# Bias rows, block sums, score rows and value banks moved in a hybrid attention and HGRN2 layer

## The chip, the cores and the metric

One core of a Trainium2 chip runs the whole layer. The metric is the device time of one execution in microseconds; before and after are compared by the median of several runs. TensorE (PE) does the products and transposes, VectorE (DVE) and ScalarE (ACT) the elementwise work, GpSimd (POOL) a few powers and the issue of some DMAs, and SyncE (SP) issues most DMAs.

## The reference

One decoder layer for x of shape (1, 1024, 1024) in float32. Cut to its core:

```python
mod = silu(c) @ w_ada + b_ada
shift, scale, gate = split(mod, 3)
h = rmsnorm(x, norm_g) * (1 + scale) + shift
q_a, k_a, v_a, z_a, q_b, f_b, i_b, z_b, g_a, g_b = split(h @ w_in)
o_a = dilated_attention(q_a, k_a, v_a, rel_bias) * silu(z_a)      # 8 heads of 64
o_b = rmsnorm(hgrn2(silu(q_b), f_b, i_b, lb), onorm_g) * silu(z_b)  # 8 heads of 128
y = sigmoid(g_a) * (o_a @ w_branch_a) + sigmoid(g_b) * (o_b @ w_branch_b)
out = rmsnorm(x + gate * (y @ w_out), final_g)
```

The attention is causal softmax attention over three dilated windows, whose outputs are merged by the weights of their softmax denominators. The kernel does this as one softmax over all earlier keys, with a bias (a bucketed `rel_bias` plus the logarithm of how many windows hold the key) that depends on the distance alone.

## The kernel before, in words

Every fp32 product is done as three fp32r products of high and low parts (`mm3`: hi x hi, lo x hi, hi x lo). h, transposed, stands in four blocks: `b11`, `b12` (upper half of the rows, first and second half of the tokens), `b21`, `b22` (lower half). Most projections go in pairs of column blocks by a Strassen-like scheme (`add_pair`: seven steps of four products of three matmuls each instead of eight), for which four sums of blocks, `t1` to `t4`, are made beforehand.

**The order of work.** PE runs in the order of the program throughout. ACT, DVE and POOL are ordered by a planner with its own costs, which may put a later instruction ahead of an earlier one when the earlier waits; the exception is a `region` at the start, in which these engines also keep the order of the program. The planner may put instructions from outside the region between those inside.

**The start (L629 to L719).** x is loaded in eight tiles. `norm_x(t)` (ACT square sum, DVE, POOL power) and `scale_x(t)` (DVE) prepare a tile; `turn_x(j, th)` transposes (PE) and copies (ACT and DVE in turn). `bias_row(b)` makes a third of the bias table by a product, `bias_add(b)` adds the logarithm on DVE, and after the third the table is stored by a DMA that ACT issues (L624). `modulate(c)` makes scale and shift of two row blocks j (PE, ACT, DVE); `make_h(j, th)` writes h's high part (ACT) and low part (DVE). `first_products(j)` adds row block j to the first three projections (q, k and v of heads 0 and 1), in six banks; `split_first(n)` makes the high and low parts of their weights in one of four buffers. `sum_1(k)` makes a slice of `t1`; `sums(k)` makes slices of `t2`, `t3` and `t4` in place and destroys what `sum_1(k)` reads. At the end `FIRST[u][1]` (`ev_q`, `ev_k`, `ev_v`) copies the banks out and stores q and k; the region closes ahead of that.

**The stream.** All other projections are `stream` steps. A step is 12 matmuls in four quarters; `stream.ahead` splits the weights of the next two steps. `fill(n)` runs as many quarters as n times `fill.rate`, up to step `fill.limit`; what the limit holds back is owed. The first two steps (`first`) are another pair of v columns, and the transposes of v come between them.

**Attention (L753 to L876).** The 32 items are (head h, row pair j), j = 0 to 3. `load_head(h)` loads q, k, v and the bias of a head. `begin(n)` is a generator that does `score(h, i)` for the two rows of item n, one for each `next`: per chunk of up to 512 keys two products into one of two banks `pss`, a DVE operation that adds the bias and finds the maximum, and then exp (ACT), reciprocal and scaling (DVE). Meanwhile the item before is worked off: for m = 0 to j `turn(h, j, m)` transposes probabilities into `pt` and splits them to `pth` and `ptl`, and one turn later `value(h, j, m)` multiplies them with v into `po`; after the last m ACT and DVE copy `po` out. Filler is placed between, weighted by `ATT_W[j]`:

```python
if j < 3 or m > 1:
    fill(0.15 * w); next(nxt, None); fill(0.3 * w)
    if j in (0, 3):
        next(nxt, None)
    fill(0.25 * w)
```

So with j = 0 and 3 both rows of the next item are begun at one m, with j = 1 and 2 at m = 0 and m = 1. Row 7 of a head also calls `load_head(h + 1)`.

**After it.** Eight loads of the attention output are gated by `z` and split into `oah` and `oal`, with `fill(6)` after each, up to step `in_gating` (14 steps past `in_attention`, which is step 85). Then comes the branch product `m<-oah`, and the recurrence with more of the stream.

Of the kernel before, what the change touches and what calls it, by code (L numbers as in the profile page):

```python
# [10 lines left out]
F32 = mybir.dt.float32  # L11
# [8 lines left out]
P = 128  # L20
# [43 lines left out]
RAW = 6  # L64
CT = 7
AHEAD = 2
ATT_W = (2.4, 1.3, 0.9, 0.7)


class Stream:  # L70
# [104 lines left out]
def hybrid_layer(ctx: ExitStack, tc: tile.TileContext, x, w_ada, b_ada, w_in, w_branch_a, w_branch_b, w_out,  # L175
# [45 lines left out]
    fill = Filler(stream)  # L221
# [262 lines left out]
    with ExitStack() as st:  # L484
# [16 lines left out]
        region = ExitStack()  # L501
# [59 lines left out]
        def split_first(n):  # L561
            hi, lo = (wpool.tile([P, 4, P], F32R, name=name) for name in ("w_hi", "w_lo"))
            nc.scalar.copy(hi, stream.tiles[ids[n]])
            sub(lo, stream.tiles[ids[n]], hi)
            stream.done(ids[n])
            firsts[n] = hi, lo
# [49 lines left out]
        def bias_row(b):  # L616
            pb = pbs[b] = pm.tile([NH, 384], F32, name=f"pm{b}_0")
            nc.tensor.matmul(pb, rb, oh[:, 384 * b:384 * b + 384], start=True, stop=True)

        def bias_add(b):  # L620
            sl = slice(384 * b, 384 * b + 384)
            nc.vector.tensor_tensor(lc[:, sl], pbs[b], lc[:, sl], ALU.add)
            if b == 2:
                nc.scalar.dma_start(toep_d, lc)  # L624
# [16 lines left out]
        junk = lp.tile([P, D], BF16, name="junk")  # L641
        rows = [lp.tile([P, 256], F32, name=f"row{a}") for a in range(2)]

        for b in range(3):
            bias_row(b)
        norm_x(0)
        norm_x(1)
        scale_x(0)
# [1 line left out]
        scale_x(1)  # L650
        norm_x(3)
        scale_x(2)
        for b in range(3):
            bias_add(b)
        norm_x(4)
        scale_x(3)
        for j in range(4):
# [10 lines left out]
        for j in range(KT):  # L668
            turn_x(j, 1)
        split_first(0)  # L670
        modulate(0)
        load_wa(2)
        main = {(u, th): pm.tile([P, 512], F32, name=f"pm{u}_{th}") for th in range(2) for u in range(3)}
        make_h(0, 0)
        split_first(1)
        make_h(0, 1)
# [4 lines left out]
            first_products(0, us=(u,))  # L681
        modulate(1)
        load_wa(3)
        first_products(1)
        for j in (2, 3):
            for th in range(2):
                make_h(j, th)
        split_first(3)
        sum_1(0)
        sum_1(1)  # L690
        first_products(2)
        modulate(2)
        modulate(3)
        lx.close()
        add_blocks(hctx.enter_context(tc.tile_pool(name="hpool2", bufs=1, reuse_waits="tile")),
                   "b21", "b22", "t2", "t3", "t4")
        first_products(3)
        for th in range(2):
            make_h(4, th)
        split_first(4)  # L700
        split_first(5)
        for u in range(3):
            first_products(4, us=(u,))
        for j in (5, 6, 7):
            for th in range(2):
                make_h(j, th)
            if j < 7:
                sum_1(j - 3)
        first_products(5)
        stream.issue()  # L710
        first_products(6)
        region.close()
        stream.ahead(0)
        for u in range(3):
            first_products(KT - 1, us=(u,))
            for th in range(2):
                FIRST[u][1](main[u, th], th, True)
        for k in range(4):
            sums(k)  # L719
    again = dict(space=PSUM, reuse_waits="tile")  # L720
# [32 lines left out]
    with ExitStack() as at:  # L753
        ap1 = at.enter_context(tc.tile_pool(name="att1", bufs=1, **right))
        ap2 = at.enter_context(tc.tile_pool(name="att2", bufs=2, **right))
        psS = at.enter_context(tc.tile_pool(name="ps_s", bufs=2, **again))
        psO = at.enter_context(tc.tile_pool(name="ps_o", bufs=1, **again))
        heads = {}

        def load_head(h):  # L760
# [50 lines left out]
            sub(ptl[:, :w], pt[:, :w], pth[:, :w])  # L811
            return pth, ptl

        pos = {}

        def value(h, j, m, parts):
            vq, hh = heads[h][4], h % 2
            if m == 0:
                pos[h, j] = psO.tile([P, 256], F32, name="po")
            po = pos[h, j]  # L820
            for kk in range(2):
                kt = 2 * m + kk
                c0, n = kk * 256, (256 if kt <= 2 * j else P)
                for a, src in enumerate(parts):
                    nc.tensor.matmul(po[:, 256 - n:256], vq[:, kt], src[:, c0:c0 + n],  # L825
                                     start=kt == 0 and a == 0, stop=kt == 2 * j + 1 and a == 1)
            if m == j:
                t1 = ap1.tile([E, 256], F32, name="t1")
                oa = ap2.tile([E, 256], F32, name="oa")
                nc.scalar.copy(t1, po[E:2 * E])  # L830
                nc.vector.tensor_tensor(oa, po[0:E], t1, ALU.add)
                nc.sync.dma_start(oa_d[h // 2][E * hh:E * hh + E, 256 * j:256 * j + 256], oa)
# [19 lines left out]
                value(*late.pop(0))  # L852

        load_head(0)
        fill.limit = in_attention
        fill.rate = in_attention * 4 / NH / sum((j + 1) * w for j, w in enumerate(ATT_W))
        for _ in begin(0):
            fill(1.0)
        for n, (h, j) in enumerate(items):
            nxt = begin(n + 1)  # L860
            for m in range(j + 1):
                late.append((h, j, m, turn(h, j, m, rows[n])))
                w = ATT_W[j]
                if j < 3 or m > 1:
                    fill(0.15 * w)
                    next(nxt, None)
                    fill(0.3 * w)
                    if j in (0, 3):
                        next(nxt, None)
                    fill(0.25 * w)  # L870
                else:
                    fill(0.7 * w)
                run_late(1)
                fill(0.3 * w)
            rows.pop(n)
# [462 lines left out]
```

## Time and profile before

| | before |
|---|---|
| median of 3 runs | 1184.62 us (1182.9 to 1187.39) |
| profiled execution | 1183.43 us, span 1181.7 us |
| PE busy | 1118.6 us, 95% of the span |
| DVE busy | 820.2 us, 69% |
| ACT busy | 561.0 us, 47% |
| DMA | 189.53 MB, mean 160 GB/s |

PE does nearly all that lies on the way to the end. Rows of the profile name an engine, a line of the kernel, and the tiles as out<-in; what stands in brackets is how long the engine had been idle and what ended that. The tile names that matter here: `pm` the six banks of the first products, `pss` scores, `pt` transposed probabilities, `po` value products, `s` a row of probabilities, `m` a product of the stream. In rows of busy time by stretch the columns are the stretch, its length, the busy time of PE, its weight loads, DVE, ACT and POOL (with their instructions), the granted PE clock, and the share and rate of the DMA engines. The execution has four places that the change touches: the start (0 to 91 us), the begin of attention (to 118 us), attention (to 476 us) and the gating behind it (to 517 us).

### The profile page before, as it was taken

What the parts mean: (1) busy time and instruction counts of PE and PEld (TensorE: products, weight loads), DVE (VectorE), ACT (ScalarE), POOL (GpSimd) and SP (SyncE); (2) the same over time, 40 slices, a digit from 0 to 9 for tenths busy, and PEclk for the clock granted to TensorE, in tenths of its full rate; (3) what the DMA queues carried; (4) which work ended last, traced back from release to release, by engine and by line L of the source; (5) the groups of instructions that cost most, each with busy time, mean ns of one, the idle gap of its engine ahead of it and who ended that gap; (6) DMA issues with size and microseconds to landing.
All of it is one profiled execution on the core that took longest, in us unless ns stands there. A gap on an engine that the chain in (4) does not pass through costs nothing.

```text
span 1181.7 us, 21561 instructions
## 1 busy us (share of the span) xinstructions
PE 1118.6 (95%) x8250; PEld 913.3 (77%) x8250; DVE 820.2 (69%) x1636; ACT 561.0 (47%) x1092; POOL 69.8 (6%) x114
## 2 busy tenths in 40 slices
PE   4998999999999998999999999999999999999997
PEld 2766878877887787878877878788787877888886
DVE  4586878877777777654778797878878673668052
ACT  4454655578898886431343434344443433223021
POOL 2001101001011010000000000000000012000000
PEclk9798999999999999999999999999999999999998
DMA  9618567465365462766726254453525369874052
GB/s 315 206 50 227 150 180 168 145 170 147 97 147 149 115 148 72 243 192 216 224 66 197 82 178 135 126 171 90 188 82 171 111 218 307 287 226 153 19 178 72
DMA packets 157751, 189.53 MB, mean 160 GB/s; under 512 B 10656, under 2 KB 107040, under 8 KB 157648
## 3 DMA queue, kind: packets, MB, share of 16 engines
q1 hardware_dynamic: 149936, 162.34, 44.4%
q0 software_dynamic: 7296, 25.17, 8.6%
q8 instruction: 65, 1.06, 0.4%
q10 hardware_dynamic: 416, 0.65, 0.2%
q14 instruction: 38, 0.31, 0.1%
HBM read 129.36 MB, written 58.76 MB: 159 GB/s over the span
## 4 chain that ended last, share of the span: by engine, by line
PE 69%; issue 8%; DMA 8%; DVE 7%; ACT 6%; POOL 1%; SPq 0%; POOLq 0%; DVEq 0%; ACTq 0%
PE m L233 14%; PE m L235 13%; PE m L234 13%; PE pq L233 5%; PE pq L234 5%; PE pq L235 5%; DMA w_raw<-in_w_in_dram 4%; DMA k<-qk_d 2%; PE pp L978 2%; PE po L825 1%; PE pt L806 1%; ACT s L794 1%; DVE w_lo L218 1%; DMA x<-in_x_dram 1%; PE pou L1042 1%
## 5 line engine op out<-in xcount | busy, mean ns | idle before, releaser
L218 DVE TENSOR_TENSOR w_lo<-w_raw,w_hi 128x512 fp32r<-128x512 f32 x156 | 106.8, 687 | 41.9 <-ACT w_hi L240 40.3
L240 ACT CAST w_hi<-w_raw 128x512 fp32r<-128x512 f32 x146 | 90.2, 621 | 91.7 <-PE m L235 54.1
L316 ACT COPY ct<-m 128x512 f32<-128x512 f32 x90 | 52.6, 584 | 90.8 <-PE m L235 87.8
L240 ACT CAST w_hi<-w_s 128x512 fp32r<-128x512 f32 x90 | 56.0, 622 | 83.0 <-PE m L235 58.3
L263 DVE TENSOR_TENSOR ct<-m,ct 128x512 f32<-128x512 f32 x90 | 61.8, 686 | 20.0 <-PE m L235 19.5
L218 DVE TENSOR_TENSOR w_lo<-w_s,w_hi 128x512 fp32r<-128x512 f32 x90 | 61.8, 686 | 8.8 <-ACT w_hi L240 8.2
L794 ACT ACTIVATE s<-s,st 128x128 f32<-128x128 f32 (+3 forms) x64 | 49.7, 776 | 27.7 <-DVE st L791 27.4
L218 DVE TENSOR_TENSOR ptl<-pt,pth 128x512 fp32r<-128x512 f32 (+1 forms) x80 | 50.5, 632 | 16.8 <-ACT pth L810 16.4
L806 PE MATMUL pt<-kc,s 128*128 128x128 f32 x288 | 47.3, 277 | 11.0 <-DVE s L796 8.5
L810 ACT CAST pth<-pt 128x512 fp32r<-128x512 f32 (+1 forms) x80 | 43.1, 540 | 23.1 <-PE pt L806 20.7
L806 PEld LDWEIGHTS pt<-kc,s 128*128 128x128 f32 x288 | 35.8, 141 | 23.5 <-DVE s L796 12.3
L233 PE MATMUL m<-b21h,w_hi 128*128 128x512 f32 x124 | 52.3, 422 | 0.0
L233 PE MATMUL m<-b11h,w_hi 128*128 128x512 f32 x124 | 52.2, 421 | 0.0
L233 PE MATMUL m<-t4h,w_hi 128*128 128x512 f32 x120 | 50.4, 420 | 0.4 <-DVE ct L263 0.4
L233 PE MATMUL m<-b22h,w_hi 128*128 128x512 f32 x124 | 50.8, 410 | 0.0
L233 PE MATMUL m<-t1h,w_hi 128*128 128x512 f32 x120 | 50.1, 418 | 0.0
L233 PE MATMUL m<-t3h,w_hi 128*128 128x512 f32 x120 | 50.1, 418 | 0.0
L233 PE MATMUL m<-t2h,w_hi 128*128 128x512 f32 x120 | 49.6, 413 | 0.0
L235 PE MATMUL m<-b11l,w_hi 128*128 128x512 f32 x124 | 49.5, 399 | 0.0
L234 PE MATMUL m<-b11h,w_lo 128*128 128x512 f32 x124 | 49.2, 397 | 0.0
L235 PE MATMUL m<-b21l,w_hi 128*128 128x512 f32 x124 | 48.8, 394 | 0.0
L235 PE MATMUL m<-b22l,w_hi 128*128 128x512 f32 x124 | 48.7, 393 | 0.0
(333 smaller groups left out, 3186.2 us busy)
## 6 DMA issues: line engine op xcount, KB each, us to landing
w_raw<-in_w_in_dram SPq DMA_DIRECT2D x128, 256.0 KB, 3.2
wa<-in_w_ada_dram SPq DMA_DIRECT2D x16, 512.0 KB, 7.7
qk_d<-ct SPq DMA_DIRECT2D x32, 256.0 KB, 3.3
k<-qk_d POOLq DMA_DIRECT2D x32, 256.0 KB, 7.5
x<-in_x_dram SPq DMA_DIRECT2D x8, 512.0 KB, 9.3
toep<-toep_d SPq DMA_DIRECT2D x8, 512.0 KB, 9.4
qp<-qk_d POOLq DMA_DIRECT2D x16, 256.0 KB, 6.1
vq_d<-ct SPq DMA_DIRECT2D x32, 128.0 KB, 4.5
```

What stands on the lines that cost most here:

```text
L218: nc.vector.tensor_tensor(out_, a, hi.bitcast(F32), ALU.subtract)
L233: nc.tensor.matmul(ps, ah, bh, start=start, stop=False, skip_group_check=more)
L234: nc.tensor.matmul(ps, al, bh, start=False, stop=False, skip_group_check=more)
L235: nc.tensor.matmul(ps, ah, bl, start=False, stop=stop, skip_group_check=more)
L240: nc.scalar.copy(hi, src)
L263: nc.vector.tensor_tensor(out_, a, b_, op)
L316: nc.scalar.copy(c[name], b[which])
L794: nc.scalar.activation(s[:, :kw], s[:, :kw], AF.Exp, bias=prev, scale=-1.0, accum_out=st2[:, 2:3])
L806: nc.tensor.transpose(pt[:, c0:c0 + P], pn[b][:, kt * P:(kt + 1) * P], ident)
L810: nc.scalar.copy(pth[:, :w], pt[:, :w])
L825: nc.tensor.matmul(po[:, 256 - n:256], vq[:, kt], src[:, c0:c0 + n], start=kt == 0 and a == 0, stop=kt == 2 * j + 1 and a == 1)
L978: nc.tensor.matmul(pl[32 * b:32 * b + 32, c], kk[:, o:o + 32], qb[:, 2 - n:2, o:o + 32], start=True, stop=True)
```

## The change

1. The three `bias_row` go from ahead of `norm_x(0)` to behind the transposes of x and the first weight split, ahead of `modulate(0)`. The three `bias_add`, with the store of the table, go behind `modulate(0)`, ahead of the first `make_h`.
2. `sum_1(0)` goes behind `modulate(3)`; `sum_1(1)` to `sum_1(3)` go behind `first_products(6)` and `stream.ahead(0)`. `make_h` of each row block stands one product earlier, and the region closes only after the first products and their copies.
3. Both score rows of the next item are begun at one m (m = 0, or m = 2 for j = 3), with `fill(0.5)` between them. `ATT_W` grows for j = 0 and 1. The limit of the filler in attention is `in_gating`, and a `fill(1.0)` stands ahead of the first scores, with 0.5 instead of 1.0 after each of the two rows.
4. `po` is one tile of one bank for all items; item (h, j) takes the half j % 2.

```diff
-ATT_W = (2.4, 1.3, 0.9, 0.7)
+ATT_W = (2.6, 1.4, 0.9, 0.7)
...
-        for b in range(3):
-            bias_row(b)
         norm_x(0)
...
-        for b in range(3):
-            bias_add(b)
...
         split_first(0)
+        for b in range(3):
+            bias_row(b)
         modulate(0)
         load_wa(2)
+        for b in range(3):
+            bias_add(b)
...
         load_wa(3)
+        for th in range(2):
+            make_h(2, th)
         first_products(1)
-        for j in (2, 3):
-            for th in range(2):
-                make_h(j, th)
+        for th in range(2):
+            make_h(3, th)
         split_first(3)
-        sum_1(0)
-        sum_1(1)
         first_products(2)
...
-        first_products(3)
+        sum_1(0)
         for th in range(2):
             make_h(4, th)
+        first_products(3)
         split_first(4)
         split_first(5)
+        for th in range(2):
+            make_h(5, th)
         for u in range(3):
             first_products(4, us=(u,))
-        for j in (5, 6, 7):
-            for th in range(2):
-                make_h(j, th)
-            if j < 7:
-                sum_1(j - 3)
+        for th in range(2):
+            make_h(6, th)
         first_products(5)
+        for th in range(2):
+            make_h(7, th)
+        first_products(6)
         stream.issue()
-        first_products(6)
-        region.close()
         stream.ahead(0)
+        for k in (1, 2, 3):
+            sum_1(k)
         for u in range(3):
             first_products(KT - 1, us=(u,))
             for th in range(2):
                 FIRST[u][1](main[u, th], th, True)
+        region.close()
...
+        po2 = psO.tile([P, 2, 256], F32, name="po2")
...
-            if m == 0:
-                pos[h, j] = psO.tile([P, 256], F32, name="po")
-            po = pos[h, j]
+            po = po2[:, j % 2]
...
-        fill.limit = in_attention
+        fill.limit = in_gating
         fill.rate = in_attention * 4 / NH / sum((j + 1) * w for j, w in enumerate(ATT_W))
+        fill(1.0)
         for _ in begin(0):
-            fill(1.0)
+            fill(0.5)
...
-                if j < 3 or m > 1:
-                    fill(0.15 * w)
+                if m == (0 if j < 3 else 2):
                     next(nxt, None)
-                    fill(0.3 * w)
-                    if j in (0, 3):
-                        next(nxt, None)
-                    fill(0.25 * w)
+                    fill(0.5)
+                    next(nxt, None)
+                    fill(0.7 * w - 0.5)
```

More of the change, by code (lines that the diff above doesn't have):

```diff
@@ L670, in hybrid_layer @@
         split_first(0)
+        for b in range(3):
+            bias_row(b)
         modulate(0)
         load_wa(2)
-        main = {(u, th): pm.tile([P, 512], F32, name=f"pm{u}_{th}") for th in range(2) for u in range(3)}
+        for b in range(3):
+            bias_add(b)
+        main = {(u, th): pm.tile([P, 512], F32, name=f"pm{u}_{th}") for th in range(2) for u in (0, 1, 2)}
         make_h(0, 0)
@@ L812, in turn @@
             return pth, ptl
-        pos = {}
         def value(h, j, m, parts):
             vq, hh = heads[h][4], h % 2
-            if m == 0:
-                pos[h, j] = psO.tile([P, 256], F32, name="po")
-            po = pos[h, j]
+            po = po2[:, j % 2]
             for kk in range(2):
```

## The prediction

> **What bounds the kernel now.** I read the page first, then the busy time by stage, then who TensorE (PE) waits for in the two stages that the change touches most. All sums are against the profiled execution: 1183.43 us with a span of 1181.7 us, 1.2 us under the median of the three runs, 1184.62 us.
>
> ```profile
> span 1181.7 us, 21561 instructions
> PE 1118.6 (95%) x8250; PEld 913.3 (77%) x8250; DVE 820.2 (69%) x1636; ACT 561.0 (47%) x1092; POOL 69.8 (6%) x114
> ...
> 75.00:118.00 43.00, 35.11 (x144) 27.56 (x144) 32.72 (x64) 21.16 (x42) 4.34 (x8) 0.88 0.64 171
> 118.00:460.00 342.00, 327.11 (x1730) 272.74 (x1729) 259.95 (x605) 251.88 (x440) 25.72 (x48) 1.00 0.55 143
> 460.00:476.00 16.00, 12.53 (x70) 10.67 (x69) 10.10 (x20) 8.06 (x14) 0.00 (x0) 0.89 0.19 58
> 476.00:517.00 41.00, 40.56 (x186) 33.45 (x185) 28.74 (x46) 20.82 (x37) 0.00 (x0) 1.00 0.75 237
> ```
>
> PE is the bound, and the change removes no product, so only idle PE (63 us of the span) and time at the half clock can be won. Idle and in reach: 7.9 us before attention (first row of stages), 14.9 us in it, 3.5 us at its end. The waits of PE in the second of these stretches, and the main one of the third:
>
> ```profile
> PE pt L806 <- DVE s L796: 8.5, 9, 1.7
> PE po L825 <- DVE oa L831: 5.3, 2, 2.9
> PE pss L789 <- DMA k<-qk_d: 0.9, 2, 0.6
> ...
> PE pt L806 <- ACT ct L460: 2.5, 1, 2.5
> ```
>
> The reader sees two different illnesses: transposes of an item that come before its softmax is done (8.5 us), and, in the last line, attention running out of interleaved projection work.
>
> **1. Bias rows behind the transposes.** The start, in order of time:
>
> ```profile
> 11.83 3.99 PE L618 MATMUL pm<-oh,rb 32*8 32x384 f32 x6 [11.83 <-DMA oh<-in_onehot_dram]
> 15.86 0.55 DVE L622 TENSOR_TENSOR lc<-pm,lc 8x384 f32<-8x384 f32 x1 [0.73 <-PE pm L618]
> 16.82 1.06 ACT L554 ACTIVATE junk<-x 128x1024 bf16<-128x1024 f32 x1 [3.72 <-DVE lc L622]
> 18.89 0.47 PE L574 MATMUL pxt<-kc,x 128*128 128x128 f32 x1 [2.24 <-DVE x L559]
> 35.49 1.07 PE L532 MATMUL pmod<-wa,scz 128*32 128x256 f32 x16
> 38.76 0.81 ACT L580 ACTIVATE b11h<-xt,mods 128x512 fp32r<-128x512 f32 x1 [0.89 <-DVE mods L545]
> ...
> L517 SPq DMA_DIRECT2D x<-in_x_dram x1: 328/328/328, 3.4 to 3.4; - x1
> DMA to landing us min/median/max: 9.7/9.7/9.7
> ...
> 1061.22 1.72 PE pq L1221 x4
> ```
>
> The norm of the fifth x tile (16.82) stands on ScalarE (ACT) behind the store of the bias table, which waits for the last bias addition on VectorE (DVE). The tile itself, issued at 3.4, landed 9.7 us later, at 13.1. Freed, the chain norm, scale, transposes moves 3.7 us forward, to the end of the transposes. But the six products then stand between the transposes and `modulate(0)`: 3.99 us as in their row, or, at full clock, 6 x 0.32 = 1.9 us by the f32 product of the last line (four records of 512 columns in 1.72 us, 0.43 each). The clock rose here just as the transposes ended, so I take 2.4. The additions now stand on DVE behind `modulate(0)` (3 x 0.55 = 1.65 us), and the store's issue, 0.28 us, stands on ACT ahead of the first `make_h`, which PE's first product waits for. Sum: -3.7 + 2.4 + 1.65 + 0.28 = +0.6 us; ends -1.6 (additions hidden) and +2.2 (products at half clock).
>
> **2. `sum_1` behind the products, the region longer, filler ahead of the first scores.**
>
> ```profile
> 85.17 0.50 PE L593 MATMUL pm<-b21l,w_hi 128*128 128x512 f32 x1 [1.36 <-DVE b21l L218]
> 92.10 1.09 ACT L380 COPY ct<-pm 128x512 f32<-128x512 f32 x2
> 96.79 1.03 PE L439 MATMUL pt<-kc,ct 128*128 128x128 f32 x8
> 108.11 0.44 PE L788 MATMUL pss<-k,qp 128*128 128x128 f32 x1 [4.83 <-DMA k<-qk_d]
> ...
> 82.80:86.20 3.40, 1.70 (x5) 0.78 (x5) 3.40 (x8) 2.54 (x5) 0.00 (x0) 1.00 0.00 0
> 86.20:89.60 3.40, 2.77 (x7) 2.19 (x8) 3.06 (x6) 1.22 (x3) 0.00 (x0) 0.51 0.41 154
> 103.30:106.70 3.40, 0.00 (x0) 0.00 (x0) 2.37 (x4) 1.45 (x3) 0.00 (x0) 1.00 1.31 229
> 106.70:110.10 3.40, 1.36 (x4) 1.14 (x5) 0.30 (x2) 0.04 (x1) 0.00 (x0) 0.51 1.12 295
> ...
> 170.68 0.39 PE L234 MATMUL m<-t1h,w_lo 128*128 128x512 f32 x1
> 170.91 0.40 PE L235 MATMUL m<-t1l,w_hi 128*128 128x512 f32 x1
> ```
>
> With `sum_1` out of the way, `make_h(7)` comes before PE needs it: the waits around 85 (1.70 us idle in their 3.4 us stretch) and the half clock that follows them (0.51, so 1.7 us) go, and with the delay in resuming PE ends the first products about 4.5 us earlier. What is late next is the copy-out of q, k and v. It is now inside the hand-ordered region, behind `stream.ahead(0)`, whose second weight split needs a buffer that the last products' first third still reads, and behind three `sum_1` of some 2 us each (DVE, ACT, DVE in series; two 128x512 copies took 1.09 us above, so 0.6 to 0.7 us a step is an estimate). So the v copy (92.10 before) falls to about 96, the k stores likewise 2 us later, and PE, 4.5 us early at the v transposes (96.79), waits there. k lands about when it did, near 108. What remains is that `fill(1.0)` puts four quarter steps into the 4.83 us wait: 4 x 0.69 = 2.8 us won (a quarter is three 128x512 products, which start 0.23 us apart by the last two rows). The clock was 0.51 after this wait; 3.4 us of products at half clock lose 1.7 us, and I count 1.0 of them as won, since PE may still be idle enough for the clock to fall. Against it, only half as much filler stands behind the second row: 1.0 us of waiting. With 0.7 us for a slightly earlier k: -2.8 - 1.0 + 1.0 - 0.7 = -3.5 us. Ends: -7 (copies not late) and +5 (DVE does its sums first, k and weights late).
>
> On the clock the rows above show PE idle for 3.40 us, then 0.51 granted; but also 1.70 us idle of 3.40, then 0.51. The Trainium skill, "TensorE: Matmul & The Clock Gate", section "What's actually happening", puts the half clock after at least one idle window of about 3.4 us. By that rule the shortened wait would keep the full clock and win the other 0.7 us; the first pair of rows disagrees with it.
>
> **3. Both score rows at the first step.** For a third or fourth item this moves the second row from the next m to the same m.
>
> ```profile
> 172.28 0.39 PE L788 MATMUL pss<-k,qp 128*128 128x512 f32 x1
> 174.27 0.35 DVE L791 CUSTOM_DVE_ANT_0 s<-pss,toep,st 128x128 f32<-128x128 f32 x1
> 177.24 0.39 PE L788 MATMUL pss<-k,qp 128*128 128x512 f32 x1
> 181.96 0.55 PE L806 MATMUL pt<-kc,s 128*128 128x128 f32 x3 [0.50 <-DVE s L796]
> ...
> 217.46 0.39 PE L788 MATMUL pss<-k,qp 128*128 128x512 f32 x1
> 220.85 0.34 DVE L791 CUSTOM_DVE_ANT_0 s<-pss,toep,st 128x128 f32<-128x128 f32 x1
> ```
>
> Here the second row started 5.0 us after the first, and its softmax came 0.50 us late. Moved to 2.1 us after it (0.75 us of products, two quarters of 0.69), it is ready nearly 3 us sooner, more than the longest such wait, 1.7. Eight of the nine waits go: 7.5 us by their mean, and 1.0 us of resuming; one, at a head's first item, stays and grows, since 0.9 instead of 1.085 units of filler follow the second row there: +1.5. The next head's loads start earlier, too: -0.9 for the k waits.
>
> The price: a row of two chunks takes both score banks. The first row's second reduction ends 2.3 us after the row's start in the first case above, 3.7 in the other. The second row needs that bank at 2.1 + 0.5 = 2.6 us. So it waits 0 to 1.2 us, sixteen times (two items in eight heads): 0 to 19 us. Most rows lie near the first case; I take 0.3 each, +5. Sum: -8.5 + 1.5 - 0.9 + 5 = -2.9 us.
>
> **4. Two half banks for the value products.** Nothing, -1 at best, no loss that I see. The halves lie in one bank, and readers of a bank wait for all its writers:
>
> ```profile
> 670.77 0.39 PE L1059 MATMUL pou<-st,qb 128*128 128x128 f32 x2
> 672.11 0.39 PE L1059 MATMUL pou<-st,qb 128*128 128x128 f32 x2
> 672.60 0.28 ACT L1062 ACTIVATE jk<-pou 128x128 f32<-128x128 f32 x1 [2.37 <-PE pou L1059]
> ```
>
> ACT, idle for 2.37 us, wanted the first quarter of that bank, done at 671.2, and started only when the fourth was written. The 5.3 us of `po` waits (two) would stay. Even apart, `ptl` stood on the same blocked DVE queue in both. The Trainium skill, "PSUM — Partial Sum Buffer", section "PSUM bank collisions raise a hardware error", asks that engines be kept apart by bank and quadrant, not by address; this trace agrees by that 2.37 us. By addresses alone the halves would win up to 5.3 us.
>
> **5. More filler at the end, less after it.** The limit was 85 steps; attention's fill calls asked for (2 + 84) x 4.05 = 348 quarters where 83 x 4 = 332 were left. Now 89.2 x 3.90 = 348, and the limit is 14 steps on. So 16 quarters, 11 us, come into attention's tail. Its 3.5 us of idle and the clock of 0.89 over 16 us (1.8 us) are covered, with resuming some 6 us: -6 (ends -6.5 and -3).
>
> Those 11 us are then missing in the next stage:
>
> ```profile
> L218 DVE TENSOR_TENSOR oal<-oar,oah x8: 683/684/693, 481.9 to 508.5; 128x512 fp32r<-128x512 f32 x8
> ...
> L233 PE MATMUL m<-oah,w_hi x64: 392/397/477, 516.8 to 561.2; 128*128 128x512 f32 x64
> ```
>
> The gated attention output is whole at 509.2; PE asks for it at 516.8, 7.6 us of slack. Minus 11 that is -3.4 us of waiting; less crowded engines may finish the loads sooner: I take +2.5 (0 to +6).
>
> **Sum.** 0.6 - 3.5 - 2.9 + 0 - 6 + 2.5 = -9.3 us: 1183.4 - 9.3 = 1174.1, 1174 us. The weight `ATT_W` moves filler between items, not its total; its cost is inside term 3.
>
> **The rivals.**
> *Everything carries through.* Copies not late (-7 instead of -3.5), score banks free in time (0 instead of +5), `oal` keeps pace (0 instead of +2.5): 1174 - 11 = 1163 us. For it: DVE is busy only 260 of 342 us in attention. Against: its queue is in order, and one reduction took 3.7 us. Chance 0.20.
> *The gain before attention isn't one.* The longer region holds q, k and v; DVE, which has 32.7 us of work in 43, does it in a worse order and attention begins later: +5 instead of -3.5, so 1182 us. For it: the split that waits for the last products stands ahead of the copies on both engines. Against: PE arrives 4.5 us early, so that much of a delay costs nothing. Chance 0.24.
> *Slower: the second rows wait for the score banks.* Place: the first m of second and third items. With a mean wait of w the time is 1174 - 5 + 16 w, which passes 0.5% above today's at w = 1.34 us; at 1.4 us it is 1191 us. For it: the 3.7 us case, and two rows at once crowd DVE's queue further. Against: that case makes 1.1 to 1.2 us, and most rows end sooner. Chance 0.13.
> My forecast has 0.43.
>
> **How the numbers follow.** A difference under 0.5%, 5.9 us, can't be told from none: faster is below 1178.7, slower above 1190.5. The forecast's own range, 1167 to 1181, puts 0.34 below 1178.7 and 0.09 in between; the first rival is faster (0.20); the second 0.04 faster, 0.18 same, 0.02 slower; the third 0.03 same, 0.10 slower. Faster 0.58, same 0.30, slower 0.12. The range reaches from just under the first rival, 1160, to the third's place, 1190.
>
> **What would show it.** Right: the fifth norm at 13 to 14 us and no gap before it; the first `b11h` at 39 to 40; no wait around 85, but one before the v transposes; filler between 103 and 108; transposes that no longer wait for `s`, and score products that wait for DVE `st` by some 5 us; `po` waits as before; no idle stretch at attention's end, and a wait of `m<-oah` for `oah`. Wrong: scores that begin after 110; score waits over 15 us; idle PE over 5 us ahead of `m<-oah`.

## The result, and the profile after

The changed kernel takes 1190.93 us (median of 20 runs, 1181.89 to 1196.4) against 1182.74 us for the kernel before, measured beside it (20 runs, 1176.92 to 1188.28). The ratio is 1.0071, interval 1.0052 to 1.0089: it is slower by 8.4 us. The forecast was 1174, with 1160 to 1190 as its range, so both the sign and the range were wrong. The profiled execution took 1191.0 us with a span of 1189.2 us.

Busy time by stage in the changed kernel, with the columns of the table shown for before, and then the waits of PE from 118 to 460 us (total, times, longest):

```profile
75.00:112.50 37.50, 31.70 (x134) 25.96 (x133) 32.62 (x61) 18.64 (x38) 3.39 (x7) 0.91 0.59 165
112.50:460.00 347.50, 328.05 (x1693) 270.27 (x1692) 254.64 (x596) 247.26 (x433) 27.69 (x50) 0.98 0.56 142
460.00:486.00 26.00, 26.00 (x148) 21.92 (x147) 19.99 (x39) 15.48 (x28) 0.00 (x0) 1.00 0.29 90
...
514.00:525.00 11.00, 6.88 (x24) 5.26 (x23) 5.44 (x9) 3.27 (x7) 0.00 (x0) 0.69 0.70 226
```

```profile
PE po L825 <- DVE oa L831: 11.8, 9, 3.1
PE pss L792 <- DVE st L795: 3.2, 5, 1.4
PE pt L810 <- DVE s L800: 2.9, 3, 1.6
```

Attention begins earlier and its end has no idle PE any more (26.00 busy of 26.00). But inside it a wait that the prediction held constant has more than doubled: `po`, 11.8 us in nine waits where before had 5.3 in two. And a new hole stands at 514 us.

Where the 7.5 us of the two profiled spans come from, by the starts of PE's instructions:

| | before | after |
|---|---|---|
| first transposition of probabilities | 118.06 | 112.54 |
| last value product | 473.87 | 486.11 |
| first product of the gated attention output | 516.82 | 524.57 |
| end of the span | 1181.7 | 1189.2 |

The first transposition comes 5.5 us earlier, but 0.7 us of that is one quarter of filler less ahead of it (69 products of the stream instead of 72): 4.8 us won. Attention is 17.8 us longer (373.6 against 355.8); it holds 48 products of the stream more (1021 against 973), by 0.23 us each some 11.0 us, so 6.8 us are lost there. The gating stage is 4.5 us shorter though 45 products, 10.3 us, left it: 5.8 us lost. -4.8 + 6.8 + 5.8 = +7.8, and what follows differs by only 0.2 us.

### The profile page after: what moved, and what is told of

Its sections match the earlier page's. It is cut to its first block, busy times and chain, and to the rows that moved or that the text cites. A ratio compares the mean times of both kernels' runs of the same rounds, so it can differ in the third digit from the quotient of the medians.

```text
span 1189.2 us, 21553 instructions
## 1 busy us (share of the span) xinstructions
PE 1122.1 (94%) x8250; PEld 914.1 (77%) x8250; DVE 820.8 (69%) x1636; ACT 559.6 (47%) x1090; POOL 70.8 (6%) x114
## 4 chain that ended last, share of the span: by engine, by line
PE 76%; DVE 8%; DMA 7%; ACT 6%; issue 3%; POOL 1%; POOLq 0%; ACTq 0%; SPq 0%; DVEq 0%
PE m L233 15%; PE m L235 14%; PE m L234 14%; PE pq L233 5%; PE pq L234 5%; PE pq L235 5%; DMA w_raw<-in_w_in_dram 3%; PE pp L977 3%; PE po L825 2%; PE pt L810 2%; DVE w_lo L218 2%; ACT L798 1%; PE pou L1041 1%; PE pou L1056 1%; PE pss L792 1%
## 5 line engine op out<-in xcount | busy, mean ns | idle before, releaser
L825 PE MATMUL po<-pth,vq 128*128 128x256 f32 (+1 forms) x160 | 41.2, 279 | 11.9 <-DVE oa L831 11.8
L234 PE MATMUL m<-b21h,w_lo 128*128 128x512 f32 x124 | 49.7, 401 | 0.0
L795 DVE CUSTOM_DVE_ANT_0 s<-pss,toep 128x512 f32<-128x512 f32 (+2 forms) x64 | 37.5, 586 | 17.0 <-PE pss L793 16.1
```

The lines of the kernel that those rows point to most:

```text
L234: nc.tensor.matmul(ps, al, bh, start=False, stop=False, skip_group_check=more)
L795: nc.vector.tensor_tensor_reduce(s[:, ks:ks + w], ps[:, :w], toep[:, x0:x0 + w][:, ::-1], -1.0, prev, ALU.add, ALU.min, st2[:, a:a + 1])
```

## The experiments

Each ratio is against runs of the kernel before on the same chip, in five rounds. First, which part carries the loss.

**start_only** has only the moved bias rows, sums and region (parts 1 and 2 of the change).

> The kernel before with the start of the change alone (bias rows, bias additions, sum_1, make_h and the longer region); attention as before. My theory, that the start gains and the loss lies in attention and behind it: PE reaches attention some 6 us earlier but waits for k until 105 to 106 us, so the first transposes of probabilities come at 114 to 116 us instead of 118; 1179 to 1181 us, 0.2 to 0.4% faster. Rival, that the copies of q, k and v, now in the region, eat the gain: first transposes at 118 or later, 1183 us, no change.

Measured: 1182.01 us, ratio 0.9985 [0.9966, 1.0005].

**rows_only** has only this:

```diff
-ATT_W = (2.4, 1.3, 0.9, 0.7)
+ATT_W = (2.6, 1.4, 0.9, 0.7)
...
-                if j < 3 or m > 1:
-                    fill(0.15 * w)
+                if m == (0 if j < 3 else 2):
                     next(nxt, None)
-                    fill(0.3 * w)
-                    if j in (0, 3):
-                        next(nxt, None)
-                    fill(0.25 * w)
+                    fill(0.5)
+                    next(nxt, None)
+                    fill(0.7 * w - 0.5)
```

> The kernel before with both score rows at one step and the new ATT_W alone. My theory, that two rows at once crowd VectorE's queue so that the copy-out of the value bank comes late: 6 to 10 waits of po for oa, 9 to 14 us of them, 3 to 5 us of waits for the score banks, the waits of pt for s down to 3 us; 1186 to 1190 us, 0.3 to 0.6% slower. Rival, that the value halves or the fill limit cause the loss: po waits stay at two and some 5 us, the pt waits go, 1177 to 1180 us.

Measured: 1191.96 us, ratio 1.0074 [1.0047, 1.0101].

**limit_only** has only the filler's limit and the filler ahead of the first scores:

```diff
-        fill.limit = in_attention
+        fill.limit = in_gating
+        fill(1.0)
         for _ in begin(0):
-            fill(1.0)
+            fill(0.5)
```

> The kernel before with the filler limit in_gating, the fill(1.0) ahead of the first scores and 0.5 behind each of the first two rows alone. My theory, that the filler is only moved: the idle end of attention goes (-5 us), PE then waits 4 to 6 us in the gating stage, partly at half clock, and 2 us are won at the first scores; 1181 to 1184 us, no change. Rival, that the gating loads keep up: 1176 us, 0.6% faster.

Measured: 1184.03 us, ratio 1.0005 [0.9984, 1.0025]. Its profiled execution, 1191.09 us, lies 7 us above that median, so I use its rows for places, not for sizes. The same holds for rows_copy_first and rows_split_load below, whose profiled executions lie 4 and 5 us under their medians, and for rows_load_later, 5 us above.

**after_no_halves** is the changed kernel with `po` as before:

```diff
-            po = po2[:, j % 2]
+            if m == 0:
+                pos[h, j] = psO.tile([P, 256], F32, name="po")
+            po = pos[h, j]
```

> The changed kernel with one value tile for each item, as before, instead of the two halves of one bank. My theory, that the halves do nothing since a bank is guarded as a whole: 1189 to 1192 us as with the change, with 8 to 11 waits of po for oa. Rival, that the halves in one tile bring the new po waits: back to two such waits, 1183 to 1186 us. If halves were guarded by address, it would be slower than the change by 3 us or more.

Measured: 1189.85 us, ratio 1.0064 [1.0040, 1.0088].

**after_without_rows** is the changed kernel with the loop and `ATT_W` of before.

> This is the changed kernel with the score rows and the weights as before: bias rows, sums, half banks and the filler's limit stay changed. If the rows alone carry the loss: 1180 to 1185 us, no slower than before by over 0.3%. Rival E (the parts collide: the filler's limit costs more once the start is earlier): 1187 to 1192 us.

Measured: 1185.01 us, ratio 1.0011 [0.9990, 1.0031]. So the two score rows at one step carry the loss: 1.0074 alone, and inside the change 1.0071 with them against 1.0011 without. The halves, the start and the limit are each not to be told from nothing.

**How two rows at one step lose time.** In rows_only the `po` waits are 12.7 us in nine. The longest is the step at which the next head's loads go out (`k`, issued by POOL). Before first, then rows_only; the first column is the start, the second the duration:

```profile
142.40 0.53 POOL L772 DMA_DIRECT2D k<-qk_d  x1 [29.63 <-PE pss L789]
142.79 0.68 DVE L218 TENSOR_TENSOR w_lo<-w_raw,w_hi 128x512 fp32r<-128x512 f32 x1
143.49 0.38 SPq L247 DMA_DIRECT2D w_raw<-in_w_in_dram  x1
152.66 0.69 DVE L263 TENSOR_TENSOR w_s<-w_raw 128x512 f32<-128x512 f32 x1 [4.60 <-DMA w_raw<-in_w_in_dram]
155.20 0.41 DVE L831 TENSOR_TENSOR oa<-po,t 64x256 f32<-64x256 f32 x1
155.66 0.39 PE L825 MATMUL po<-pth,vq 128*128 128x256 f32 x1 [2.37 <-DVE oa L831]
```

```profile
140.74 0.52 POOL L772 DMA_DIRECT2D k<-qk_d  x1 [29.07 <-PE pss L789]
141.25 0.75 DVE L791 CUSTOM_DVE_ANT_0 s<-pss,toep,st 128x512 f32<-128x512 f32 x1
143.66 0.75 DVE L796 TENSOR_SCALAR s<-s,st 128x1024 f32<-128x1024 f32 x1
145.16 0.68 DVE L218 TENSOR_TENSOR w_lo<-w_raw,w_hi 128x512 fp32r<-128x512 f32 x1
145.87 0.38 SPq L247 DMA_DIRECT2D w_raw<-in_w_in_dram  x1
154.81 0.69 DVE L263 TENSOR_TENSOR w_s<-w_raw 128x512 f32<-128x512 f32 x1 [6.31 <-DMA w_raw<-in_w_in_dram]
157.35 0.41 DVE L831 TENSOR_TENSOR oa<-po,t 64x256 f32<-64x256 f32 x1
157.81 0.58 PE L825 MATMUL po<-pth,vq 128*128 128x256 f32 x1 [3.88 <-DVE oa L831]
```

Read it from the top. A weight block of the stream is asked for when a raw buffer comes free, that is when its `w_lo` has been made on DVE. In rows_only the second row's work (141.25, 143.66) stands on DVE ahead of that `w_lo`, and the same second row, which is row 7 of the head, sends the next head's loads out earlier. So the weight load goes out 5.1 us behind the first of those loads instead of 1.1, 2.4 us later than in before, and lands nine microseconds after that, at 154.8; in before, too, it took nine. DVE's first use of it, `w_s`, waits 6.31 us, and in DVE's queue the copy-out `oa` stands behind `w_s`; the next value product needs the bank that `oa` empties. The chain was there before too, with 2.37 us at its end instead of 3.88; two rows lengthen it. The clock then adds to it. The stretches around this wait in before and in rows_only:

```profile
155.89:159.30 3.41, 3.41 (x24) 3.09 (x24) 3.38 (x7) 1.10 (x2) 0.00 (x0) 1.00 0.58 181
159.30:162.72 3.42, 3.42 (x21) 2.83 (x20) 3.13 (x12) 2.45 (x7) 0.00 (x0) 1.00 0.52 153
```

```profile
155.89:159.30 3.41, 1.49 (x7) 1.49 (x8) 3.41 (x7) 0.64 (x2) 0.00 (x0) 0.50 0.10 22
159.30:162.72 3.42, 3.42 (x12) 2.84 (x11) 2.35 (x6) 1.40 (x4) 0.00 (x0) 0.50 0.47 135
```

In rows_only both stretches ran at half the clock: in the second PE was busy throughout and started 12 products instead of 21. Its attention has three stretches of 3.41 us more at 0.50 than before's: at most 5.1 us lost, and by the distances between the starts of its products an estimated 4 to 5 of the 9.8 us by which its attention is longer.

Two theories were left. A: DVE's queue, with two rows ahead of the copy-out, is enough. B: it is the weight load, late behind the next head's loads, that makes the queue stand still. Three runs changed the order.

**rows_copy_first**:

```diff
                     fill(0.5)
+                    run_late(1)
                     next(nxt, None)
```

> This is rows_only with one line more: the late value step runs between the two score rows of an item's first step, so that the copy-out of po stands on DVE ahead of the second row's reductions. Theory A (rows_only loses because po's copy-out queues behind two rows on DVE, 12.7 us of po waits against 5.3 before, and the half clock that these bring): the po waits between 118 and 460 us fall to 6 to 8 us, at most one half-clock stretch of 3.4 us is left there, and the time is 1183 to 1187 us, 0.4 to 0.8% under rows_only. Rival B (the load of the next head is issued one step earlier and holds up the weight load behind it, whatever the order of the copy-out): the po waits stay over 11 us with their two long ones, and the time stays at 1190 to 1193. Rival C (the value products now come ahead of the second row's scores, and the row itself is late): pt waits grow from 2.9 to over 8 us, and the time is 1188 to 1195.

Measured: 1187.89 us, ratio 1.0040 [1.0021, 1.0059]: about half of the loss is back, but none of the three expectations is met. There are only three `po` waits instead of nine, yet they sum to 10.6 us, the longest 4.0, and DVE waits 27.1 us for `w_raw`. The many small waits were the order; the long ones were not.

**rows_load_later**:

```diff
-                    if i == 7 and h + 1 < NH:
-                        load_head(h + 1)
...
+                elif j == 2 and m == 1 and h + 1 < NH:
+                    fill(0.15 * w)
+                    load_head(h + 1)
+                    fill(0.55 * w)
```

> This is rows_only with the next head's loads put back where they stood before, at the second step of the third item instead of its first. Rival B (the earlier burst of q, k and the table delays w_raw, DVE's wait for it stands ahead of the copy-out): DVE's waits for w_raw between 118 and 460 us go from 21.3 us back to about 15, the longest po wait from 3.9 to under 3, and the time is 1184 to 1188. Theory A (DVE's queue holds two rows ahead of the copy-out, and the load's place is a detail): the time is 1190 to 1193 and the po waits are 11 to 13 us as in rows_only.

Measured: 1194.58 us, ratio 1.0112 [1.0088, 1.0137]. This did not try B, as its trace shows: the first load went out at 141.61 instead of 140.74 us, and the weight load at 146.75 instead of 145.87, so it was still 5.1 us behind. A load's place in the program did not hold it back: the first of them left when PE's scores were done.

**rows_old_weights** takes back `ATT_W` alone in rows_only.

> This is rows_only with the weights of the items as before, (2.4, 1.3, 0.9, 0.7): only the place of the score rows is changed. Theory A and rival B give both the same: 1189 to 1193 us, since the weights only shift filler between steps. Rival D (the weights carry the loss: more filler beside the first item and less beside the long ones, so that PE runs out of filler there): 1181 to 1185 us, and po waits under 8 us.

Measured: 1195.20 us, ratio 1.0103 [1.0080, 1.0125], with 18.6 us of `po` waits. The new weights are no cause of the loss; the runs differ by 0.3%, with intervals that overlap.

Then the loads themselves.

**rows_no_reload** and **before_no_reload** leave the loads of q, both k and the table for heads 1 to 7 out of both loops; these heads then compute with head 0's:

```diff
+            if h == 0:
                 qp, k1, k2 = (ap1.tile([P, S], F32R, name=n) for n in ("qp", "k1", "k2"))
                 toep = ap1.tile([P, S], F32, name="toep")
+            else:
+                qp, k1, k2, toep, _ = heads[0]
...
-            for hh in range(2):
+            for hh in range(2 if h == 0 else 0):
```

> This is rows_only without the loads of q, both k and the table for heads 1 to 7: these heads use head 0's, so that only the value block is still loaded and 2.0 MB per head are left out. It tells the late weights from the two rows in DVE's queue. Theory B' (the loss is made by the weight load that queues behind the next head's loads: 6.3 us of DVE's wait before w_s at the step that both rows now share): against before_no_reload it is within 0.3%, its po waits between 118 and 460 us are under 6 us and no half clock is left in the attention. Theory A (two rows stand in DVE's queue ahead of the copy-out of po, loads or not): it is 4 to 8 us slower than before_no_reload, with po waits of 8 to 13 us.

> This is the kernel before with the same loads left out (q, k and the table of heads 1 to 7), to be compared with rows_no_reload. Its two po waits, 5.3 us, stood behind the late weights, so both theories expect them gone: the time is 3 to 6 us under before, 1177 to 1180 us. If it is no faster than before, the loads cost the kernel before nothing.

Measured: 1175.93 us, ratio 0.9954 [0.9934, 0.9975], and 1173.63 us, ratio 0.9927 [0.9899, 0.9955]. Without the reloads the rows cost 1.0027 (0.999 to 1.006, the two intervals taken as independent) instead of 1.0074. The waits of `po`, and DVE's for the weights, in rows_no_reload:

```profile
PE po L829 <- DVE oa L835: 4.0, 6, 1.0
...
DVE w_s L263 <- DMA w_raw<-in_w_in_dram: 6.7, 8, 3.3
```

No wait of `po` is longer than 1.0 us, and between the first transposition and 460 us the clock is nowhere at half. before_no_reload has no `po` wait at all: there, too, the loads had cost time.

**rows_act_out** asks whether the bank's release or the queue is late:

```diff
                 nc.scalar.copy(t1, po[E:2 * E])
-                nc.vector.tensor_tensor(oa, po[0:E], t1, ALU.add)
+                nc.scalar.copy(oa, po[0:E])
+                nc.vector.tensor_tensor(oa, oa, t1, ALU.add)
```

> This is rows_only with po emptied by ScalarE alone: both halves are copied out by ScalarE, and VectorE adds them in SBUF, so that the bank comes free without VectorE's queue. Theory A and B' both say that po's wait for VectorE goes; what is told apart is whether the value products then run or wait for the next thing in the same queue. If the bank's release carried the loss, po waits in the attention fall from 12.7 to under 4 us and the time is 1183 to 1186 us. If the queue itself is late, the wait moves to ptl (the low part of the transposed weights, on the same engine): the waits of po stay over 8 us with ptl as their end, and the time is 1188 to 1192 us.

Measured: 1188.51 us, ratio 1.0061 [1.0037, 1.0085]. Its waits:

```profile
PE po L825 <- DVE ptl L218: 8.2, 3, 3.9
PE pt L806 <- DVE s L796: 3.9, 4, 2.5
PE pss L788 <- DVE st L791: 3.7, 5, 1.7
PE po L825 <- ACT oa L831: 0.6, 3, 0.3
```

ScalarE frees the bank in time (0.6 us), and the same product then waits for `ptl`, which stands in the same VectorE queue. The queue is late, not the bank.

Could the loads be mended with nothing left out? **rows_split_load** and **before_split_load** send each head's `q`, `k` and table in two halves:

```diff
-                nc.gpsimd.dma_start(qp[o], qk_d[4 * p + hh][r].bitcast(F32R))
+                nc.gpsimd.dma_start(qp[o, c], qk_d[4 * p + hh][r, c].bitcast(F32R))
...
+                if (j, m) == (3, 1) and h + 1 < NH:
+                    load_cols(h + 1, 1)
```

> This is rows_only with each head's loads in two halves of 512 columns: q, both k and the table's first half go out where they stood, the second half and the value block at the second step of the item after it. Nothing is left out. Theory B' (the weight load queues behind the next head's loads, and VectorE's queue behind the weights): half of the bytes stand ahead of the weight load, DVE's wait for w_raw between 118 and 460 us falls from 21.3 us to 8 to 14, the po waits from 12.7 to 4 to 8, and the time is 1183 to 1187 us. Rival A (two rows in VectorE's queue alone): po waits stay over 10 us and the time at 1190 to 1193. Rival F (the second half comes too late or stands in the same way a step later): new waits of the scores for k, or the same w_raw wait at another step, and 1188 to 1195.

> This is the kernel before with the same split of the loads, for comparison with rows_split_load. By B' its two po waits (5.3 us) fall to 1 to 3 us: 1177 to 1181 us; by rival F it is within 2 us of before or slower. The rows change then costs 2 to 4 us between the two, as it did without the reloads.

Measured: 1191.14 us, ratio 1.0104 [1.0069, 1.0140], and 1175.88 us, ratio 0.9958 [0.9935, 0.9981]. The split helps the old loop and not the new one. In rows_split_load DVE still waits 19.5 us for `w_raw` and PE 9.5 us for `po`: the weight load landed at 149.8, still too late. The order of the issues in rows_split_load says why:

```profile
138.53 0.53 POOL L779 DMA_DIRECT2D k<-qk_d  x1 [26.75 <-PE pss L796]
142.29 0.53 POOL L778 DMA_DIRECT2D qp<-qk_d  x1
143.66 0.38 SPq L247 DMA_DIRECT2D w_raw<-in_w_in_dram  x1
```

The second half was not held back by its later place in the program. It left right behind the first, from 142.29, so nine of the twelve half loads of q and k, and both halves of the table, stood ahead of the weight load. In before_split_load the weight load went out at 141.35, 1.1 us behind the first half load (140.29) and ahead of the table; it landed 4.3 us later, not 6.1, and DVE did not wait for it. So the run did not halve the bytes ahead of the weights in the new loop and could not tell A from B. Against before_split_load the rows cost 1.5%, twice what they cost without the split: only the old loop got its weights out early and was rid of its `po` waits.

**rows_raw7** and **before_raw7** ask for the weights earlier:

```diff
-RAW = 6
-CT = 7
+RAW = 7
+CT = 6
```

> This is rows_only with seven raw weight buffers instead of six (and six of the tiles for evictions instead of seven, for the space), so that a weight block is asked for about one block earlier. Nothing is left out. Theory B'' (the second row's work on VectorE frees the raw buffer later, the weight load goes out 5 us behind the next head's loads and VectorE's queue stands for it): the load now goes out ahead of the head's loads, DVE's wait for w_raw between 118 and 460 us falls from 21.3 us to under 10, po waits from 12.7 to under 7, and it is 0 to 4 us slower than before_raw7. Rival A (the crowded queue alone): po waits stay over 10 and it is 7 to 10 us slower than before_raw7.

> This is the kernel before with the same seven raw buffers and six tiles for evictions. By B'' its two po waits (5.3 us) go with the late weights: 1176 to 1181 us, if the tile missing for evictions costs nothing; if that costs (ScalarE and VectorE wait for a free tile), 1182 to 1190.

Measured: 1181.30 us, ratio 1.0001 [0.9977, 1.0026], and 1178.35 us, ratio 0.9977 [0.9956, 0.9997]. The waits of PE in rows_raw7 from 118 to 460 us:

```profile
PE pss L788 <- DVE st L791: 4.4, 9, 1.0
PE pt L806 <- DVE s L796: 2.9, 3, 1.6
PE po L825 <- DVE oa L831: 2.5, 5, 1.0
PE po L825 <- DVE ptl L218: 0.5, 1, 0.5
```

With one more raw buffer the same two rows at one step cost 1.0024 (0.999 to 1.006), not 1.0074: `po` waits 3.0 us instead of 12.7, none over 1.0, and no half clock from the first transposition to 468 us. DVE's waits for `w_raw` that are over 0.7 us are two, 0.85 and 1.00; one more idle time of 3.5 us ahead of `w_s` ends in something the profile does not name. My expectation said that the load would go out ahead of the head's loads. It did not: one still went out at 149.0 and landed at 156.0, but DVE no longer needed it then. By these two pairs, rows_no_reload and rows_raw7 each against its partner, some 6 of the 8.8 us go with the late weights (B). That is an estimate with wide intervals; the 2 to 3 us that are left in both pairs, A's share, can't be told from nothing.

Last, versions meant to gain. **start_two_steps** and **two_steps_split_load** have the start of start_only and keep the old loop; the second also has the split loads:

```diff
-        fill.limit = in_attention
+        fill.limit = in_attention + 2
```

> This is start_only (the moved bias rows and sums, without the rows change) with the filler's limit two steps later, not all of the two pairs: 8 of the 15 quarters are spent in the attention's tail, 7 stay for the gating stage. From the numbers of start_only and limit_only: the tail's idle time falls by 4 to 5 us, the gating stage loses 1 to 3 us, so 1178 to 1182 us, 0.1 to 0.4% under before. If the gating stage's wait grows to the 4 us and the half clock that limit_only showed, it is 1183 to 1186.

> This is start_two_steps with the split loads. If the two gains add up: 1173 to 1177 us, 0.4 to 0.7% under before. If the split gives nothing: 1177 to 1179 as start_two_steps.

Measured: 1177.77 us, ratio 0.9960 [0.9937, 0.9983], and 1171.74 us, ratio 0.9925 [0.9901, 0.9950]. The second is faster than both kernels, by 0.5 to 1.0% against before. The waits of PE in it from 118 to 460 us have no `po` and no `k`:

```profile
PE pt L816 <- DVE s L806: 8.5, 9, 1.7
PE pt L816 <- DVE ptl L218: 0.3, 1, 0.3
```

**after_two_steps_split** is the changed kernel with both edits.

> This is the changed kernel whole, with the limit two steps past the attention's share instead of all of it and with the split loads. By B' what made it slow is gone but for the score banks and the crowded queue (2 to 4 us): 1176 to 1181 us. If the rows cost as much as in the changed kernel: 1184 to 1188.

Measured: 1188.14 us, ratio 1.0070 [1.0040, 1.0100], with 12.5 us of `po` waits, where I had expected 1176 to 1181. It is 1.5% over two_steps_split_load, from which it differs by the rows, and also by the half banks and the filler ahead of the first scores. Here, too, the weight load (142.15) went out 5.4 us behind the first half load and was waited for, 4.75 us.

## Why the prediction was wrong, by its own steps

**Term 1, bias rows (+0.6): its mechanism held.** The rows that it named, in the changed kernel:

```profile
14.22 1.06 ACT L554 ACTIVATE junk<-x 128x1024 bf16<-128x1024 f32 x1
30.54 2.10 PE L618 MATMUL pm<-oh,rb 32*8 32x384 f32 x6
37.54 0.81 ACT L580 ACTIVATE b11h<-xt,mods 128x512 fp32r<-128x512 f32 x1 [2.60 <-DVE lc L622]
38.41 0.50 PE L590 MATMUL pm<-b11h,w_hi 128*128 128x512 f32 x1 [2.81 <-ACT b11h L580]
```

The fifth norm runs at 14.22 with no gap, the products take 2.1 us (I took 2.4), the additions are not hidden (`b11h` waits for `lc`). The first product, 38.41, is 1.2 us earlier, not 0.6 later; but it lies anywhere from 37.2 to 40.3 us in the profiles of these kernels. The seven with the new start have a mean of 39.2, the thirteen with the old one 38.6: about the 0.6 that I had, but too close for the spread to show it.

**Term 2, sums and region (-3.5): its places held.** PE waits ahead of the v transposes, as foreseen, and hardly for k:

```profile
94.19 1.97 PE L439 MATMUL pt<-kc,ct 128*128 128x128 f32 x8 [3.62 <-ACT ct L380]
105.63 0.30 PE L792 MATMUL pss<-k,qp 128*128 128x128 f32 x1 [1.24 <-DMA k<-qk_d]
106.86 0.30 PE L793 MATMUL pss<-k,qp 128*128 128x128 f32 x1 [0.93 <-DMA k<-qk_d]
```

With term 1 the first transposition of probabilities came 5.5 us earlier where I had 2.9. Most of it is the filler, not the start: limit_only's, with the old start, came at 112.69, start_only's at 116.15, and the ten profiles with the old start and neither the new filler nor split loads lie between 113.8 and 119.7. The second rival, by which attention begins later, is refuted by these places; whether the start alone gains anything stays open, in them and in the time of start_only, 0.8 us under before.

**Term 3, both rows at one step (-2.9): this step failed.** rows_only measures +8.8 us, so it was out by 11.7, enough by itself to turn the sign. Its counted parts were sound, in the changed kernel's profile: the waits for `s` fell from 8.5 to 2.9 us, with three kept (I had -8.5 and +1.5, with one kept); the k waits of attention went (-0.9); the waits for the score banks came, 3.2 us in five (I took 5 in sixteen). What failed is the sentence that `po` waits would be as before. I had even noted that `ptl` stood on the same blocked DVE queue, but priced no second row in that queue, nor what stood behind its blocking: +6.5 us of `po` waits (+7.4 in rows_only), and the half clock after them.

I counted what the moved rows do to score banks and forgot what the moved step issues besides: it sends the next head's loads out earlier and holds up the instruction that frees the weight buffer. I booked the earlier loads as a gain of 0.9.

**Term 4, half banks (0): right.** after_no_halves is at 1.0064 and the change at 1.0071; their `po` waits are 12.6 and 11.8 us.

**Term 5, the limit (-6 + 2.5): right in both places, too good in the second.** The end of attention has no idle PE. What was missing behind it:

```profile
515.68 0.69 DVE L890 TENSOR_TENSOR oar<-oar,z 128x512 f32<-128x512 f32 x1 [0.62 <-DMA oar<-oa_d]
518.10 0.68 DVE L263 TENSOR_TENSOR ct<-m,ct 128x512 f32<-128x512 f32 x1
518.92 0.76 PE L233 MATMUL m<-t4h,w_hi 128*128 128x512 f32 x1 [4.12 <-DVE ct L263]
...
514.01:517.42 3.41, 0.79 (x6) 0.46 (x4) 2.79 (x5) 1.44 (x3) 0.00 (x0) 1.00 0.95 302
517.42:520.83 3.41, 1.91 (x5) 1.55 (x6) 2.65 (x5) 1.24 (x3) 0.00 (x0) 0.50 0.66 204
520.84:524.25 3.41, 3.41 (x10) 2.53 (x9) 0.00 (x0) 0.00 (x0) 0.00 (x0) 0.50 0.64 222
```

The wait came not at `m<-oah` but at the last filler ahead of it: the copy-out of a bank stood on DVE behind gating multiplies that waited for their DMA. It was 4.1 us, and 6.8 us at half clock followed: 5.8 lost where I had 2.5, inside my bounds of 0 to 6. limit_only shows the sum: 1.0005, where I had -3.5 us. There, and in after_without_rows, the wait did stand at `m<-oah`, with 5.3 and 4.4 us. Two steps instead of all keep some filler for the gating: start_two_steps.

**Terms 1, 2, 4 and 5 together.** They add up to -6.4, and after_without_rows, which has just these, measures +1.3 us (-1.2 to +3.7). So apart from term 3 the forecast was some 8 us too good. In the changed kernel's profile the gating wait and its half clock are 3.3 us of this (term 5); the rest was not traced to a step.

**The rivals.** The third named the right time, 1191 us, and nearly the right place, but not the cause: it needed sixteen waits for score banks of 1.4 us, and there were five, 3.2 us together. That its number came out is luck. Its remark that two rows crowd DVE's queue was the right thread, and got no price of its own. The first fell with term 3.

## What to carry to other kernels

Before moving a step, list what stands behind each of its instructions in every in-order queue: not only who reads its result, but which buffer release comes later for it, and which load that release sends out. A wait on a load in such a queue holds up everything behind it, so the price of two more operations there is the distance by which the next load misses its slot, not their own duration. The place of a load in the program is not its time of issue either: look in the trace at what its queue waited for. A buffer more for the late load can be worth more than a new order: one raw weight buffer took back, by estimate, two thirds of the loss.

## What the runs showed of the hardware

A wait can cost the clock or not, by where it falls. In the 20 profiles the granted clock changes only at the borders of windows of 3.41 us: every half-clock stretch but the one that runs past the end is one or two such windows long. The borders differ from one execution to the next. In the changed kernel the wait that `oa` ended at 154.44 us was 2.92 us long, and 2.25 us of it lie in one window. PE was busy for the other 1.16 us of that window, and the next window got half the clock. In before the wait that ended at 155.66 us was 2.37 us long and is cut in two halves by a border. Both windows kept more than 2 us of work, and no half clock followed. The changed kernel first, then before:

```profile
152.19:155.60 3.41, 1.16 (x10) 1.16 (x11) 3.41 (x7) 0.62 (x1) 0.00 (x0) 1.00 0.08 23
155.61:159.03 3.42, 3.42 (x13) 2.84 (x12) 2.72 (x7) 1.60 (x4) 0.00 (x0) 0.50 0.40 109
```

```profile
151.12:154.53 3.41, 2.17 (x12) 1.46 (x10) 1.84 (x3) 1.22 (x3) 0.00 (x0) 1.00 1.18 237
154.54:157.95 3.41, 2.29 (x15) 2.12 (x16) 3.38 (x7) 1.10 (x2) 0.00 (x0) 1.00 0.77 238
```

Counted over all 20 profiles, between 118 and 560 us and in windows at full clock: all 31 with less than 1.5 us of PE's work were followed by half the clock, 12 of 23 with 1.5 to 1.8 us, and none of 2479 with more. What decides between 1.5 and 1.8 us stays open. So the clock's share of a loss in a single profile, the 4 to 5 us of rows_only too, hangs in part on where its borders fell.

The Trainium skill, "TensorE: Matmul & The Clock Gate", section "What's actually happening", asks for at least one idle window of about 3.4 us; the 2.92 us wait, which brought half the clock, is shorter.
